# A two-layer decoder trunk on one core: waits moved between ScalarE, VectorE and GpSimd in the mixer

## The chip, the cores and the metric

The kernel runs on one core of a Trainium2 chip. A core has five engines, each with its own in-order queue of instructions: TensorE (PE in the profile; its weight loads are PEld), VectorE (DVE), ScalarE (ACT), GpSimd (POOL) and SyncE (SP, which here only issues loads). They wait for one another by semaphores. Matrix products are written to PSUM banks, and PSUM is emptied by DVE or ACT. The metric is the time on the device of one execution, in microseconds (us); lower is better.

## The reference

A decoder trunk of 2 layers on 256 tokens of width 1024, everything in float32. Each layer is x + half a SwiGLU, then a mixer, then x + half a second SwiGLU:

```python
for l in range(DEPTH):
    x = x + 0.5 * swiglu_ffn(x, ffn1_norm[l], ffn1_w_gu[l], ffn1_w_down[l])      # 1024 -> 2 x 2816 -> 1024
    h = rms_norm(x, mix_norm[l])
    x = x + hybrid_mixer(h, ...)
    x = x + 0.5 * swiglu_ffn(x, ffn2_norm[l], ffn2_w_gu[l], ffn2_w_down[l])
# hybrid_mixer: h @ w_in, cut into columns for three causal attentions
o_a = stick_breaking_attention(...)   # 4 heads
o_b = nsa_attention(...)              # 8 query heads, 2 kv groups: compressed, selected and window branches
o_c = dsa_attention(...)              # 4 query heads, one kv head; relu indexer of 8 heads picks 64 keys a token
merged = g_a * (o_a @ w_br_a) + g_b * (o_b @ w_br_b) + g_c * (o_c @ w_br_c)      # g = sigmoid(h @ w_gate)
return merged @ w_out
```

Queries and keys of NSA and DSA are normalized per head (an RMS norm over 64 columns) and get a rotation on their first 16 columns; the indexer's queries and key get a rotation on 8 of 32 columns, without a norm.

## The kernel before, in words

The activations lie transposed (128 features by 256 tokens a tile). Every weight matrix streams through once in **units** of 128x1024: SP loads a unit into one of four `raw` buffers, ACT rounds it to a high part `wh` (L242), DVE, or for some units GpSimd, subtracts to get a low part `wl` (L244), and PE multiplies with both. PE's work of a unit is written two units after its load is (`LA = 2`): `unit` appends it to `ahead`, `run_unit` takes it from there.

The order of each engine is the order in which the program writes instructions, somewhat rearranged by the scheduler of the framework; PE's own order is pinned by `nosync` links, one matmul after the other. Between units run **threads**: Python generators that `spawn` registers and that `tick` resumes once a unit; `yield n` means to write on after n units. So a `yield` isn't a wait of the chip: it sets how many units' instructions stand between two pieces of a thread.

In the mixer the units are, in this order (`ORDER`): group 0 of w_in (indexer, DSA's value), the compressed keys' two units, group 3 (keys and DSA's queries), a gate pair, group 4 (NSA's queries `q8`), a gate pair, group 1 (stick-breaking's q and k, `p4`), group 2, then the rest of the gates. A group of w_in needs two `acc` banks of PSUM, a gate one; there are three `acc` banks, two `sc` (scores), two `tp` (transposes and small sums) and one `o`.

The threads that matter here: `indexer` (scores by matmuls, relu L742 on ACT into `rl`, weighted sums `isc` on DVE L746 and L748, then eight rounds of MAX and MATCH_REPLACE, L757 and L758, on both token halves); `keys` and `queries` (`norm_rope`: squares on ACT, their sums on DVE, a root by `head_rsqrt` as a logarithm and an exponential on ACT, L501, with a Newton step on DVE; two multiplications on DVE, L676 and L679; then `rope`: three products L648 to L650, of which L649 is on GpSimd, and a sum L652). `keys` then splits each key in two parts (`stack_k`: ACT L699, GpSimd L700), transposes them on PE and copies them out (`kSW` L784 on ACT, `kD` by `evens` on ACT L635 or DVE L637). `queries` does that with L880 (ACT) and L881 (DVE). `group` empties the `acc` banks (L526 on ACT: `p4` of group 1). `dsa` and `nsa_unit` are the attentions over these, written into the gates' units. `first_norm` and `norm_rstd` make the first norm's 1/rms: sums by a matmul, a root on DVE, a broadcast by a second matmul of `dg`.

The list `slow` names the units of a mixer, counted from its first, whose `wl` GpSimd makes.

Of the kernel before, what the change touches and what calls it, by code (L numbers as in the profile page):

```python
# [9 lines left out]
F32 = mybir.dt.float32  # L10
# [4 lines left out]
ALU = mybir.AluOpType  # L15
AX = mybir.AxisListType

P = 128
D = 1024
S = 256  # L20
NT = 2
# [93 lines left out]
M0 = 7  # L115
FY2 = 2
ACC = 3
SC = 2
TP = 2
# [4 lines left out]
def decoder_trunk(ctx: ExitStack, tc: tile.TileContext, x_in, consts, gains, hgain, gu1, dn1, win, wkc, wgate, cw1, cw2,  # L124
# [17 lines left out]
    def nm(s):  # L142
        cnt[0] += 1
        return f"{s}_{cnt[0]}"
# [243 lines left out]
    def rsqrt(src, n, inv):  # L388

        u, y, w = (small.tile([P, 32], F32, tag=t, bufs=2, name=nm(t))[:, 0:n] for t in "uyw")  # L390
        V.tensor_scalar(out=u, in0=src, scalar1=inv, scalar2=EPS, op0=ALU.mult, op1=ALU.add)
        V.tensor_scalar(out=y.bitcast(I32), in0=u.bitcast(I32), scalar1=-0.5, scalar2=float(0x5f3759df), op0=ALU.mult,
                        op1=ALU.add)
        for _ in range(3):
            V.tensor_tensor(out=w, in0=y, in1=y, op=ALU.mult)
            V.scalar_tensor_tensor(out=w, in0=w, scalar=-0.5, in1=u, op0=ALU.mult, op1=ALU.mult)
            V.scalar_tensor_tensor(out=y, in0=w, scalar=1.5, in1=y, op0=ALU.add, op1=ALU.mult)
        return y
# [91 lines left out]
    def mixer(l, nrm, nxt):  # L490
# [47 lines left out]

        gate, iw = st([NT, 24], "gate", 2, "gate"), st([NT, 8], "iw", 2, "iw")
        rq = st([NT], "rq", 2, "rq")  # L540
# [99 lines left out]
        def rope(v, nh, half, cs, sn):  # L640
# [7 lines left out]
            V.tensor_tensor(out=a, in0=v[:, :, :, 0:2 * half], in1=cb, op=ALU.mult)  # L648
            G.tensor_tensor(out=b[:, :, :, 0:half], in0=v[:, :, :, half:2 * half], in1=sb[:, :, :, 0:half], op=ALU.mult)  # L649
            V.tensor_tensor(out=b[:, :, :, half:2 * half], in0=v[:, :, :, 0:half], in1=sb[:, :, :, half:2 * half],  # L650
# [3 lines left out]
        def head_rsqrt(ss, n):  # L654

            u, y, w = (st([32], t, 2, t)[:, 0:n] for t in "uyw")
            V.tensor_scalar(out=u, in0=ss, scalar1=1.0 / HD, scalar2=EPS, op0=ALU.mult, op1=ALU.add)
            act_exp(out=y, in_=u, func=AF.Ln)
            act_exp(out=y, in_=y, scale=-0.5)
# [5 lines left out]
        def norm_rope(v, nh, gs, t0=0):  # L665

            nt = v.shape[1]
            ss = st([32], "hs", 2, "hs")[:, 0:nt * nh]
            for t in range(nt):
                sq = b4("sq")[:, 0:nh * HD].rearrange("p (h d) -> p h d", d=HD)  # L670
                A.activation(out=sq, in_=v[:, t], func=AF.Square)
                V.tensor_reduce(out=ss[:, t * nh:(t + 1) * nh], in_=sq, axis=AX.X, op=ALU.add)
            yield 1
            r = head_rsqrt(ss, nt * nh).rearrange("p (a b) -> p a b", b=nh)
            yield 1
# [127 lines left out]
        def compress():  # L803
# [49 lines left out]
            A.activation(out=junk, in_=kc, func=AF.Square, accum_out=css)  # L853
            yield 1
            rc = head_rsqrt(css, 1)
            V.scalar_tensor_tensor(out=kc, in0=kc, scalar=rc, in1=hg[:, 5 * HD:6 * HD], op0=ALU.mult, op1=ALU.mult)
# [17 lines left out]
        def queries():  # L874
            yield from need(4)
            parts = [norm_rope(q8[t][:, :, HD:P].unsqueeze(1), 8, ((0, 8, 3),), t) for t in range(NT)]
            for _ in zip(*parts):
                yield 1
            for t in range(NT):
                A.activation(out=q8[t][:, :, 0:HD].bitcast(F32R), in_=q8[t][:, :, HD:P], func=AF.Copy)  # L880
                V.tensor_tensor(out=q8[t][:, :, HD:P], in0=q8[t][:, :, HD:P], in1=q8[t][:, :, 0:HD], op=ALU.subtract)  # L881
            yield 4
            for t in range(NT):
# [54 lines left out]
        def dsa():  # L938
            yield from need("mdsa", "qD")
            for t in range(NT):  # L940
# [11 lines left out]
                yield 1  # L952
                o = psum("tp", TP)
                for b in range(t + 1):
# [142 lines left out]
        gates = iter(range(12))  # L1097
        slow.extend(int(u in (10, 14, 18, 27)) for u in range(62))
        for g in ORDER:
# [75 lines left out]
    def first_norm():  # L1175
        for m in range(KD):
# [3 lines left out]
            if m == 6:  # L1180
                nc.sync.dma_start(out=cst, in_=consts)
        yield 2
        yield from norm_rstd(nrm, FY2)
# [83 lines left out]
```

## Time and profile before

| | us |
|---|---|
| median of three runs | 1226.95 (1223.9 to 1229.97) |
| the profiled execution: its time | 1228.48 |
| its span, first to last instruction | 1226.7 |
| PE busy in the span | 1206.3 |
| DVE, ACT, POOL busy | 886.6, 697.6, 163.4 |
| loads: 209 MB read, mean | 171 GB/s |

A row of the order of time reads: start, duration, engine, line, operation, result <- operands, shape, count of merged instructions, and in brackets how long the engine was idle before it and what ended that. Matmuls overlap, so the next row of PE starts some 0.25 us before the end that is shown for the one before. A row of stretches gives, for each engine, busy time and in brackets the count, and then PE's granted clock (1.00 is full).

### The profile page before, as it was taken

How to read it: one execution, taken by the hardware profiler on the slowest of the kernel's cores; microseconds unless marked ns; L12 is line 12 of the kernel's file. 1: busy time of each engine (PE TensorE's matmuls, PEld its weight loads, DVE VectorE, ACT ScalarE, POOL GpSimd, SP SyncE). 2: the span in 40 equal slices, each digit the busy share in tenths (PEclk: the TensorE clock that was granted, in tenths of full speed). 3: DMA queues.
4: the chain of work that ended last, by engine and by line, in shares of the span. 5: the costliest groups of instructions: out<-in, count | busy, mean ns of one | idle time of the engine just before them, and what ended most of it. 6: DMA issues, size and time to landing. Idle time of an engine off the chain costs nothing.

```text
span 1226.7 us, 20872 instructions
## 1 busy us (share of the span) xinstructions
PE 1206.3 (98%) x7878; PEld 1075.5 (88%) x7878; DVE 886.6 (72%) x1563; ACT 697.6 (57%) x1261; POOL 163.4 (13%) x195
## 2 busy tenths in 40 slices
PE   8999999989999999999999999999999999999998
PEld 7888888878989988888888888897798899888887
DVE  7766677896766877766777766778877578776664
ACT  6655555555666565555556555545556745655542
POOL 2111011330000111110111110122300001111100
PEclk9999999999999999999999999999999999999999
DMA  7555566644334565556656655665433346555563
GB/s 265 178 188 184 179 188 193 213 145 131 106 102 141 177 193 191 191 185 182 189 182 196 191 186 184 191 197 192 139 127 112 104 148 195 181 192 190 186 198 104
DMA packets 60885, 212.09 MB, mean 173 GB/s; under 512 B 6992, under 2 KB 8048, under 8 KB 60784
## 3 DMA queue, kind: packets, MB, share of 16 engines
q1 hardware_dynamic: 60192, 209.65, 53.7%
q0 software_dynamic: 448, 1.08, 0.4%
q8 instruction: 62, 1.02, 0.3%
q14 instruction: 39, 0.32, 0.1%
q10 hardware_dynamic: 144, 0.02, 0.0%
HBM read 209.15 MB, written 1.05 MB: 171 GB/s over the span
## 4 chain that ended last, share of the span: by engine, by line
PE 89%; DVE 6%; DMA 2%; ACT 1%; POOL 1%; issue 1%; SPq 0%; ACTq 0%; DVEq 0%; POOLq 0%
PE acc L196 67%; PE sc L196 17%; PE tp L689 2%; DVE wl L244 2%; PE o L196 1%; DMA raw<-in_win 1%; DVE isc L758 1%; PE tp L196 1%; DVE m L757 1%; ACT wh L242 1%; DVE isc L748 1%; DMA gn<-in_gains 0%; POOL rb L649 0%; DVE p L679 0%; DVE isc L746 0%
## 5 line engine op out<-in xcount | busy, mean ns | idle before, releaser
L242 ACT ACTIVATE wh<-raw 128x1024 fp32r<-128x1024 f32 (+4 forms) x402 | 412.1, 1027 | 412.4 <-PE acc L196 285.6
L244 DVE TENSOR_TENSOR wl<-raw,wh 128x1024 fp32r<-128x1024 f32 (+3 forms) x394 | 468.3, 1191 | 221.5 <-ACT wh L242 220.4
L196 PE MATMUL acc<-aT,wh 128*128 128x512 f32 (+1 forms) x1696 | 414.1, 342 | 1.1 <-ACT wh L242 1.1
L196 PEld LDWEIGHTS acc<-aT,wh 128*128 128x128 f32 x1696 | 264.9, 189 | 41.0 <-ACT wh L242 1.5
L196 PE MATMUL acc<-aT,wl 128*128 128x256 f32 x1280 | 297.1, 280 | 0.7 <-DVE wl L244 0.7
L196 PE MATMUL acc<-hT,wh 128*128 128x512 f32 (+1 forms) x792 | 239.1, 369 | 0.0
L196 PEld LDWEIGHTS acc<-aT,wl 128*128 128x128 f32 x1280 | 215.9, 189 | 3.0 <-DVE wl L244 2.0
L196 PE MATMUL sc<-aT,wh 128*128 128x512 f32 x544 | 190.8, 395 | 0.0
L196 PE MATMUL acc<-hT,wl 128*128 128x256 f32 x704 | 186.6, 283 | 0.0
L196 PEld LDWEIGHTS acc<-hT,wh 128*128 128x128 f32 x792 | 137.4, 188 | 26.9
L196 PE MATMUL sc<-aT,wl 128*128 128x256 f32 x544 | 150.6, 278 | 0.0
L196 PEld LDWEIGHTS acc<-hT,wl 128*128 128x128 f32 x704 | 127.1, 188 | 0.0
L442 POOL TENSOR_TENSOR v<-v,R 128x256 f32<-128x256 f32 x88 | 68.2, 779 | 414.3 <-DVE v L358 359.9
L196 PEld LDWEIGHTS sc<-aT,wh 128*128 128x128 f32 x544 | 101.8, 188 | 23.6
L196 PEld LDWEIGHTS sc<-aT,wl 128*128 128x128 f32 x544 | 102.3, 188 | 0.4
L386 POOL TENSOR_TENSOR ssum<-ssum,sq 128x256 f32<-128x256 f32 x42 | 38.3, 912 | 449.1 <-ACT sq L385 448.9
L196 PE MATMUL acc<-wh,aT 128*128 128x512 f32 (+1 forms) x320 | 83.9, 404 | 4.6 <-ACT p L526 4.6
L196 PEld LDWEIGHTS acc<-wh,aT 128*128 128x128 f32 x320 | 59.3, 194 | 15.9 <-ACT p L526 5.5
L357 ACT ACTIVATE half<-acc 128x256 f32<-128x256 f32 x136 | 49.4, 365 | 2.6 <-PE acc L196 1.8
L444 DVE TENSOR_TENSOR v<-v,v 128x256 f32<-128x256 f32 x88 | 38.4, 440 | 12.1 <-ACT v L443 4.3
L376 DVE SCALAR_TENSOR_TENSOR aT<-x,gn,aT 128x256 fp32r<-128x256 f32 x48 | 40.5, 853 | 6.9 <-ACT aT L375 6.9
L501 ACT ACTIVATE E<-sc,mx 128x128 f32<-128x128 f32 (+1 forms) x80 | 32.6, 418 | 21.8 <-DVE mx L905 21.7
(241 smaller groups left out, 1262.8 us busy)
## 6 DMA issues: line engine op xcount, KB each, us to landing
raw<-in_gu SPq DMA_DIRECT2D x175, 512.0 KB, 3.7
raw<-in_dn SPq DMA_DIRECT2D x64, 512.0 KB, 3.5
raw<-in_wgate SPq DMA_DIRECT2D x48, 512.0 KB, 3.4
raw<-in_win SPq DMA_DIRECT2D x32, 512.0 KB, 3.5
raw<-in_dn SPq DMA_DIRECT2D x32, 384.0 KB, 3.0
raw<-in_wbr SPq DMA_DIRECT2D x16, 512.0 KB, 3.4
raw<-in_wout SPq DMA_DIRECT2D x16, 512.0 KB, 3.5
raw<-in_cw SPq DMA_DIRECT2D x8, 512.0 KB, 4.5
```

The lines of the kernel that those rows point to most:

```text
L196: return pe(T.matmul(o, lhsT=lhsT, rhs=rhs, start=start, stop=stop, skip_group_check=True))
L242: A.activation(out=wh[:, w], in_=raw[:, w], func=AF.Copy)
L244: e.tensor_tensor(out=wl[:, w], in0=raw[:, w], in1=wh[:, w].bitcast(F32), op=ALU.subtract)
L357: A.activation(out=t, in_=b[:, S:2 * S], func=AF.Copy)
L376: V.scalar_tensor_tensor(out=dst[:, m, 1], in0=xs[m], scalar=g[:, m:m + 1], in1=dst[:, m, 0].bitcast(F32), op0=ALU.mult, op1=ALU.subtract)
L386: G.tensor_tensor(out=ssum, in0=ssum, in1=sq, op=ALU.add)
L442: G.tensor_tensor(out=g, in0=g, in1=N["R"], op=ALU.mult)
L444: V.tensor_tensor(out=u, in0=u, in1=g, op=ALU.mult)
L501: e = A.activation(func=func, **kw)
L689: pe(T.transpose(tp[:, b * P:(b + 1) * P], src, ident))
L748: V.scalar_tensor_tensor(out=isc[t], in0=rl[:, j], scalar=w, in1=isc[t], op0=ALU.mult, op1=ALU.add)
L757: V.max(out=m8, in_=isc[t])
```

## The change

Six edits.

1. `head_rsqrt` becomes a generator with a `yield 1` behind the scaled sum u (L657): the logarithm and the exponential on ACT are written one unit later than u. In `norm_rope` and `compress` the `yield 1` that stood ahead of u goes. The buffers of u, y and w become 3, 4 and 2 of 18 columns (2 of 32 before).
2. `queries`: two units (`yield 2`) more stand ahead of the copies and subtractions (L880, L881), two less behind them.
3. `rope`: the first of the two sine products (L649) goes from GpSimd to DVE.
4. `dsa`: the sums over the values go to an `acc` bank instead of a `tp` bank.
5. `slow`: of four units of a mixer (10, 14, 18, 27) only 27 keeps its `wl` on GpSimd.
6. The first norm: one unit less ahead of its sum's matmul (`yield 1`), one more between that and the broadcast (`FY2 = 3`).

```diff
-FY2 = 2
+FY2 = 3
...
-        u, y, w = (small.tile([P, 32], F32, tag=t, bufs=2, name=nm(t))[:, 0:n] for t in "uyw")
+        u, y, w = (small.tile([P, 18], F32, tag=t, bufs={'u': 3, 'y': 4, 'w': 2}[t], name=nm(t))[:, 0:n] for t in "uyw")
...
-        gate, iw = st([NT, 24], "gate", 2, "gate"), st([NT, 8], "iw", 2, "iw")
+        gate, iw = st([NT, 24], "gate", 1, "gate"), st([NT, 8], "iw", 1, "iw")
...
-            G.tensor_tensor(out=b[:, :, :, 0:half], in0=v[:, :, :, half:2 * half], in1=sb[:, :, :, 0:half], op=ALU.mult)
+            V.tensor_tensor(out=b[:, :, :, 0:half], in0=v[:, :, :, half:2 * half], in1=sb[:, :, :, 0:half], op=ALU.mult)
...
         def head_rsqrt(ss, n):
 
-            u, y, w = (st([32], t, 2, t)[:, 0:n] for t in "uyw")
+            u, y, w = (st([18], t, {'u': 3, 'y': 4, 'w': 2}[t], t)[:, 0:n] for t in "uyw")
             V.tensor_scalar(out=u, in0=ss, scalar1=1.0 / HD, scalar2=EPS, op0=ALU.mult, op1=ALU.add)
+            yield 1
             act_exp(out=y, in_=u, func=AF.Ln)
...
                 V.tensor_reduce(out=ss[:, t * nh:(t + 1) * nh], in_=sq, axis=AX.X, op=ALU.add)
-            yield 1
-            r = head_rsqrt(ss, nt * nh).rearrange("p (a b) -> p a b", b=nh)
+            r = (yield from head_rsqrt(ss, nt * nh)).rearrange("p (a b) -> p a b", b=nh)
...
-            yield 1
-            rc = head_rsqrt(css, 1)
+            rc = yield from head_rsqrt(css, 1)
...
             for _ in zip(*parts):
                 yield 1
+            yield 2
             for t in range(NT):
                 A.activation(out=q8[t][:, :, 0:HD].bitcast(F32R), in_=q8[t][:, :, HD:P], func=AF.Copy)
                 V.tensor_tensor(out=q8[t][:, :, HD:P], in0=q8[t][:, :, HD:P], in1=q8[t][:, :, 0:HD], op=ALU.subtract)
-            yield 4
+            yield 2
...
-                o = psum("tp", TP)
+                o = psum("acc", ACC)
...
-        slow.extend(int(u in (10, 14, 18, 27)) for u in range(62))
+        slow.extend(int(u == 27) for u in range(62))
...
-        yield 2
+        yield 1
         yield from norm_rstd(nrm, FY2)
```

How the instructions move on the engines, at three places of the first mixer (the second is alike). ACT's queue at the indexer's second token half (`rl` is the relu of a bank of scores, `kk` the high part of the split keys, `hs` an exponential of the compressed keys):

```order
-L699 ACTIVATE kk_2712<-p_401_2152 128x4x128
 L742 ACTIVATE rl_2675<-sc_2672 128x512
 L742 ACTIVATE rl_2682<-sc_2679 128x512
 L501 ACTIVATE hs_519_2688<-o_2448 128x60
+L699 ACTIVATE kk_2712<-p_401_2152 128x4x128
 L699 ACTIVATE kc_524_2715<-p_401_2152 128x128
```

The split of the keys moved behind two relus and the exponential.

ACT's queue from the roots of the compressed keys and the queries (`y`) to the emptying of group 1 (`p`), before:

```order
L242 ACTIVATE wh_2926<-raw_2924 128x1024
L501 ACTIVATE y_2804<-u_2803 128x1
L501 ACTIVATE y_2804<-y_2804 128x1
L242 ACTIVATE wh_2970<-raw_2968 128x1024
L501 ACTIVATE y_2861<-u_2860 128x8
L784 ACTIVATE kSW_2164<-tp_2944 128x4x128
L501 ACTIVATE y_2861<-y_2861 128x8
L784 ACTIVATE kSW_2164<-tp_2950 128x4x128
L242 ACTIVATE wh_3005<-raw_3003 128x1024
```

and with the change:

```order
L242 ACTIVATE wh_2926<-raw_2924 128x1024
L501 ACTIVATE y_2758<-u_2757 128x1
L501 ACTIVATE y_2804<-u_2803 128x8
L501 ACTIVATE y_2812<-u_2811 128x8
L501 ACTIVATE y_2758<-y_2758 128x1
L501 ACTIVATE y_2804<-y_2804 128x8
L501 ACTIVATE y_2812<-y_2812 128x8
L242 ACTIVATE wh_2970<-raw_2968 128x1024
L784 ACTIVATE kSW_2164<-tp_2944 128x4x128
L784 ACTIVATE kSW_2164<-tp_2950 128x4x128
L242 ACTIVATE wh_3001<-raw_2999 128x1024
```

The six roots stand together ahead of one wh, and the two copies of keys behind it. Further on, the query copies (L880) stand a place earlier against the wh's: the second one, which stood right ahead of the four p's (L526), has now one wh between itself and them.

DVE's queue from the first to the second sum of the queries' rotation (L652 of `q_402` and `q_403`, the two token halves), before:

```order
L637 CAST kD_2165<-tp_2986 128x2x128
L660 TENSOR_TENSOR w_2871<-y_2870 128x8
L648 TENSOR_TENSOR ra_2956<-q_402_2153,cst 128x128
L661 SCALAR_TENSOR_TENSOR w_2871<-w_2871,u_2869 128x8
L650 TENSOR_TENSOR rb_2957<-q_402_2153,cst 128x8x8
L662 SCALAR_TENSOR_TENSOR y_2870<-w_2871,y_2870 128x8
L244 TENSOR_TENSOR wl_3006<-raw_3003,wh_3005 128x1024
L676 TENSOR_TENSOR q_403_2154<-q_403_2154,y_2870 128x8x64
L652 TENSOR_TENSOR q_402_2153<-ra_2956,rb_2957 128x8x16
L679 TENSOR_TENSOR q_403_2154<-q_403_2154,hg_2139 128x8x64
L244 TENSOR_TENSOR wl_3034<-raw_3031,wh_3033 128x1024
L648 TENSOR_TENSOR ra_2962<-q_403_2154,cst 128x128
```

and with the change:

```order
L650 TENSOR_TENSOR rb_2957<-q_402_2153,cst 128x8x8
L244 TENSOR_TENSOR wl_2971<-raw_2968,wh_2970 128x1024
L652 TENSOR_TENSOR q_402_2153<-ra_2956,rb_2957 128x8x16
L637 CAST kD_2165<-tp_2986 128x2x128
L648 TENSOR_TENSOR ra_2962<-q_403_2154,cst 128x128
L649 TENSOR_TENSOR rb_2963<-q_403_2154,cst 128x8x8
L650 TENSOR_TENSOR rb_2963<-q_403_2154,cst 128x8x8
L244 TENSOR_TENSOR wl_3002<-raw_2999,wh_3001 128x1024
L652 TENSOR_TENSOR q_403_2154<-ra_2962,rb_2963 128x8x16
L244 TENSOR_TENSOR wl_3030<-raw_3027,wh_3029 128x1024
L881 TENSOR_TENSOR q_402_2153<-q_402_2153 128x8x64
L881 TENSOR_TENSOR q_403_2154<-q_403_2154 128x8x64
```

With the change kD, an emptying of a transpose bank, stands behind a wl and the sum of the first half; L649 is in the queue; the Newton steps (L660 to L662, with the change L661 to L663), which stood between the pieces of the rotation, come earlier; one wl instead of two stands between the two sums, and both subtractions (L881) stand behind the second sum, the first one no longer ahead of it. Three pairs of the top-k's rounds (`m_608` and `m_609` the first of them), which stood further up in this queue, follow behind L881.

More of the change, by code (lines that the diff above doesn't have):

```diff
@@ L667, in norm_rope @@
             nt = v.shape[1]
-            ss = st([32], "hs", 2, "hs")[:, 0:nt * nh]
+            ss = st([18], "hs", 2, "hs")[:, 0:nt * nh]
             for t in range(nt):
```

## The prediction

> **What bounds the kernel now.** I read the busy line first, then the stretches, then TensorE's (PE's) order of time at the waits, then the queue that each wait leads to.
>
> ```profile
> PE 1206.3 (98%) x7878; PEld 1075.5 (88%) x7878; DVE 886.6 (72%) x1563; ACT 697.6 (57%) x1261; POOL 163.4 (13%) x195
> ```
>
> PE sets the end, so only PE's lost time can be won. The stretches (columns: start:end, length, then busy us and count of PE, weight loads, DVE, ACT, POOL; then granted clock, DMA share, GB/s) say where it is lost:
>
> ```profile
> 20.00:135.00 115.00, 114.03 (x649) 98.83 (x648) 83.25 (x144) 69.03 (x126) 15.65 (x21) 1.00 0.59 189
> 232.70:275.50 42.80, 38.50 (x232) 31.83 (x232) 42.17 (x113) 24.14 (x48) 15.64 (x12) 1.00 0.51 166
> 300.00:383.00 83.00, 82.25 (x718) 75.99 (x719) 54.14 (x114) 56.31 (x131) 0.00 (x0) 1.00 0.37 117
> 838.30:881.10 42.80, 39.23 (x226) 32.27 (x224) 42.21 (x112) 24.46 (x48) 15.70 (x12) 0.96 0.52 168
> ```
>
> In the FFN and in the attention PE has no gap worth a term (bar one of about 1 us in each). In 43 us of each mixer it idles, and there DVE is the full engine: 42.2 of 42.8 us. PE's order of time there, first mixer, then second:
>
> ```profile
> 240.13 2.07 PE L196 MATMUL acc<-wh,aT 128*128 128x512 f32 x8
> 244.54 0.51 PE L196 MATMUL sc<-ikS,iqS 128*128 128x256 f32 x2 [1.44 <-ACT rl L742]
> 248.73 2.10 PE L196 MATMUL acc<-wh,aT 128*128 128x512 f32 x8
> 251.59 1.03 PE L689 MATMUL tp<-cst,kk 128*128 128x128 f32 x8
> 252.38 2.16 PE L196 MATMUL acc<-aT,wh 128*128 128x256 f32 x16
> 255.33 0.38 PE L689 MATMUL tp<-cst,kc 128*128 128x128 f32 x2
> 265.91 0.44 PE L689 MATMUL tp<-cst,kc 128*128 128x128 f32 x2 [0.93 <-ACT kSW L784]
> 276.93 1.94 PE L196 MATMUL acc<-wh,aT 128*128 128x512 f32 x6 [2.31 <-ACT p L526]
> 283.69 1.04 PE L689 MATMUL tp<-cst,q 128*128 128x128 f32 x8
> ...
> 845.31 2.09 PE L196 MATMUL acc<-wh,aT 128*128 128x512 f32 x8
> 850.19 0.51 PE L196 MATMUL sc<-ikS,iqS 128*128 128x256 f32 x2 [1.88 <-ACT rl L742]
> 882.56 2.93 PE L196 MATMUL acc<-wh,aT 128*128 128x512 f32 x6 [2.31 <-ACT p L526]
> 889.14 1.03 PE L689 MATMUL tp<-cst,q 128*128 128x128 f32 x8
> ```
>
> An undisturbed unit of 512 columns (12 matmuls) takes 248.73 to 251.59, 2.86 us; eight transposes 0.79; a gate unit 252.38 to 255.33, 2.95. From 240.13 to 283.69 stand nine such units, two gate units, two eights of transposes and seven small groups (some 2.3 us together, by 0.3 to 0.4 each): 25.7 + 5.9 + 1.6 + 2.3 = 35.5. PE took 43.56: **8.1 us lost**. The same work in mixer two took 43.83: **8.3 lost**. Idle time alone is less, since a waiting row costs some 0.25 beyond what is shown idle, and since part is lost at a lower clock:
>
> ```profile
> 240.57:243.98 3.41, 2.53 (x12) 1.76 (x10) 3.31 (x6) 0.61 (x2) 1.27 (x2) 1.00 0.57 193
> 274.70:278.12 3.42, 1.19 (x5) 1.02 (x6) 3.21 (x8) 2.57 (x6) 0.46 (x1) 1.00 0.50 158
> 278.12:281.53 3.41, 3.41 (x10) 2.65 (x9) 0.89 (x2) 1.06 (x1) 0.00 (x0) 0.50 0.49 156
> 848.14:851.56 3.42, 1.54 (x8) 1.21 (x8) 3.27 (x6) 2.54 (x6) 1.83 (x2) 1.00 0.44 144
> 851.56:854.97 3.41, 3.41 (x11) 2.67 (x10) 3.41 (x9) 1.98 (x3) 0.32 (x1) 0.50 0.35 135
> 878.86:882.28 3.42, 1.15 (x7) 0.69 (x6) 3.21 (x9) 2.41 (x6) 1.93 (x1) 1.00 0.73 253
> 882.28:885.69 3.41, 3.13 (x7) 2.49 (x8) 1.50 (x3) 1.61 (x5) 0.00 (x0) 0.50 0.50 160
> ```
>
> Three times 3.41 us at half clock follow 3.41 us in which PE was busy 1.2 to 1.5; after 2.53 busy none follows. They hold 10, 11 and 7 matmuls where 14.3 fit at 2.86 for twelve: at 0.238 each 1.0, 0.8 and 1.7 us. So the 16.4 hold about 3.5 that comes from the clock.
>
> **The change part by part.** Each wait is a queue standing behind ACT:
>
> ```profile
> 243.37 0.63 ACT L699 ACTIVATE kk<-p 128x512 fp32r<-128x512 f32 x1 [3.05 <-DVE p L652]
> 265.16 0.21 ACT L501 ACTIVATE y<-u 128x8 f32<-128x8 f32 x1 [3.44 <-DVE c2s L856]
> 275.52 0.63 ACT L880 ACTIVATE q<-q 128x512 fp32r<-128x512 f32 x1 [1.01 <-DVE q L652]
> 276.06 0.46 ACT L526 ACTIVATE p<-acc,rq 128x256 f32<-128x256 f32 x1
> ```
>
> *Wait at 244.54.* The indexer's relu (L742), which frees the score bank, stood behind the key split L699, which waits for the rotation's last sum (L652). In the new order two relus and the exponential stand ahead of L699: the relu needs only matmuls that end before 240.13, PE comes at 243.1, the wait is gone. Queued behind L699 is now the wh of a gate unit, due on PE some 6 us later.
>
> *Wait at 265.91.* ACT stood at a root (L501) until DVE came to its sum (u, L657); behind it stood the kSW copy that frees a transpose bank. Now all three u's stand on DVE ahead of their roots, right behind a unit's wl, and ACT comes to the six roots with the kSW copies behind them: gone, if DVE is on time.
>
> *Wait at 276.93.* PE needs the bank that p (L526) empties; p stood behind the second half's query copy (L880), that one behind L652 on DVE, whose end is 275.5. This chain stays, so DVE's sum decides. Rows for it:
>
> ```profile
> 222.13 0.29 DVE L746 TENSOR_SCALAR isc<-rl,iw 128x128 f32<-128x128 f32 x1 [2.17 <-ACT rl L742]
> 223.16 2.42 POOL L244 TENSOR_TENSOR wl<-raw,wh 128x1024 fp32r<-128x1024 f32 x1
> 231.66 1.06 ACT L242 ACTIVATE wh<-raw 128x1024 fp32r<-128x1024 f32 x1 [1.69 <-DMA raw<-in_win]
> 239.14 2.35 DVE L746 TENSOR_SCALAR isc<-rl,iw 128x256 f32<-128x256 f32 x1
> 242.48 0.29 DVE L650 TENSOR_TENSOR rb<-p,cst 128x144 f32<-128x144 f32 x1
> 253.85 0.61 DVE L757 MAX8 m<-isc 128x8 f32<-128x128 f32 x2
> 255.02 0.61 DVE L757 MAX8 m<-isc 128x8 f32<-128x128 f32 x2
> ...
> 846.79 0.34 DVE L746 TENSOR_SCALAR isc<-rl,iw 128x256 f32<-128x256 f32 x1
> L244 DVE TENSOR_TENSOR wl<-raw,wh 128x1024 fp32r<-128x1024 f32 x10 | 12.4, 1240 | 1.7 <-ACT wh L242 1.7
> ```
>
> Between the wl at 232.7 and that L652 the new order differs so. Added: wl of units 14 and 18 from GpSimd, while the wl of a later unit moves behind: one net, 1.2. Three first halves of rotations (L649) by L650's row, 0.29 and twice half of it: 0.5. Gone: L746 took 2.35 beside GpSimd's unit and 0.34 in the other mixer, where L679 met it instead: 2.0. Of the top-k, two rounds of both halves and most of a third move behind L652; a round is 253.85 to 255.02, 1.17, so 3.1; they are needed only by the DSA scores, behind all of this. The first half's subtraction (L881) moves behind: 0.9 with its wait; the wait for GpSimd's rotation, 0.2. And the start: DVE stands idle 2.17 before 222.13, so unit 10's wl is done there by about 222.6 instead of 225.6 on GpSimd; its raw buffer, and SP's queue behind it, get free 3 us sooner, and the wh of 231.66, which waited 1.69 for that load, can start up to 1.7 sooner (bounds 0 and 1.7; I take 1.6, since three us of head start exceed the wait). Sum: 275.5 - 1.6 + 1.2 + 0.5 - 2.0 - 3.1 - 0.9 - 0.2 = 269.4. Then ACT's copy, one wh and two p's, 2.0: PE goes on at 271.4. By its own work PE, with the earlier waits gone, is there at about 270.2. So 1.2 of the 8.1 stay: the gain is 6.9. Mixer two starts its DVE chain about 0.3 later against PE: 8.3 - 1.5 = 6.8. With 1.2 late the gate windows stay over 2 us busy: no half clock.
>
> GpSimd keeps at most 15.6 less two units of 2.4, 10.8 us, in this stretch (and loses its rotations). How much of it DVE will wait out isn't shown; it lies between none, with which PE waits for nothing, and all. Of what it meets now only the 2.0 at L746 goes; what is left, 1.5 at most by the other long rows there, stays in my sum, since the same key splits stay on GpSimd.
>
> **The small edits**, each bounded by its own wait:
>
> ```profile
> 29.86 0.70 PE L196 MATMUL tp<-dg,cst 128*128 128x256 f32 x2 [0.97 <-DVE dg L409]
> 362.14 0.66 PE L689 MATMUL tp<-cst,E 128*128 128x128 f32 x4 [0.75 <-ACT PT L929]
> ```
>
> The first norm's sums come a unit (2.8 us) earlier, their broadcast stays: 1.0 won; GpSimd's chain of squares ends before that unit begins, so nothing new is late. DSA's sums leave the transposes' two banks: 0.75 and 0.15 of tail in each mixer, 1.8; the product bank taken is asked for again two gate units later, 5.9 us, and is emptied by four short copies. Buffers of u, y, w, gate, iw: nothing; three roots of y and two of u are live at once in the new order and find three and four. Sum: 6.9 + 6.8 + 1.0 + 1.8 = 16.5, at most 19.2. From the profiled execution's 1228.48: 1212.0. The median of the three runs stands 1.5 below it, so 1210.5 to 1212: **1211**.
>
> **The rivals.** *DVE takes PE's waits (0.18).* For: it is full, and two-input operations beside GpSimd ran long (L746, L679). Against: most of them didn't. Half of GpSimd's 10.8 met instead of 1.5 delays PE by 3.9 in each mixer: 16.5 - 7.8 gives 1219. By the Trainium skill, "SBUF — State Buffer", section "Who interferes with whom", a VectorE instruction with two SBUF inputs shares GpSimd's read port, an exclusive lock: that speaks for this rival.
>
> *The half clock stays (0.10).* Then its 3.5 us aren't the waits' doing: 16.5 - 3.5 gives 1214. For: it would need another cause, such as power; against: all three follow an idle stretch. The Trainium skill, "TensorE: Matmul & The Clock Gate", section "HAM oscillation — how this bites in real kernels", asks for "no PE-idle gaps >~3.4µs": by that rule these gaps, 2.3 us at most, wouldn't close the gate. The trace differs: it closed after 1.9 to 2.3 idle in 3.41.
>
> *Slower (0.05).* One mechanism: DVE's chain to L652 ends later than 275.5 instead of 269.4. It takes over 6.1 more on DVE. All of GpSimd's 10.8 met adds 9.3, to 278.7: PE then waits 3.2 longer than now in each mixer, and only the small edits are won: 1228.5 + 6.4 - 2.8 = 1232. It decides from 275.5 on, that is when DVE waits out some two thirds of GpSimd's time.
>
> *The waits only move (0.04).* The loads bound the stretch, and PE stands for raw tiles instead: near 1226. Against: DMA share 0.51 there, and only the wh's of 231 to 237 waited for loads.
>
> **How the numbers follow.** Forecast 0.63, the rest as above. Its own range is 1207.5 (all 19.2 won, less 1.5) to 1215 (no earlier load, 1.6 twice). Taking in the half clock and DVE's case with 2 us behind it, and 1 us of spread below: 1206.5 to 1221. A measurement of this kernel tells 0.5% (6.1 us), so faster means under 1220.8: 0.63 + 0.10 + 0.12 of the 0.18 make 0.85; same 0.10; slower 0.05.
>
> **What would show it.** Right: the waits on rl, kSW and dg gone from PE's rows, the one on p at most 1.5; three clock stretches of 0.50 gone; L746 near 0.34; DVE still full from 232 to 270 and the top-k's last rounds behind it; the second DSA wait gone. Wrong: PE waiting for kD (L637), which now stands behind a unit and half the rotations on DVE and holds a transpose bank: due at 267.5 by the sum, asked at 266.4, inside the 1.2 above. If that wait exceeds 3 us, or the hrep sums come after 246, my order of DVE was too short.

## The result and the profile after

The changed kernel takes 1207.2 us (median of four runs, 1206.65 to 1211.23) against 1228.1 (1223.9 to 1229.97): the ratio is 0.9842, with a 95% interval of 0.9807 to 0.9876. It is faster, by about 19 us after the ratio (20.9 between the medians); 1211 was forecast, in a range of 1206.5 to 1221. Its profiled execution is the slowest of its four, 1211.23 with a span of 1209.5, against 1228.48 and 1226.7 before. So the two traces differ by 17.2 us, and that is what can be followed in them.

The busy line of the changed kernel:

```profile
PE 1197.8 (99%) x7878; PEld 1070.7 (89%) x7878; DVE 884.2 (73%) x1577; ACT 697.9 (58%) x1261; POOL 145.8 (12%) x181
```

PE is now idle for 11.7 us of the span instead of 20.4. The stretches that answer to those of before, each mixer's full part from the unit ahead of it (columns as before: length, busy us of PE, weight loads, DVE, ACT, POOL, then granted clock, DMA share, GB/s):

```profile
20.00:135.00 115.00, 114.55 (x652) 99.31 (x651) 82.49 (x144) 69.42 (x127) 18.36 (x22) 1.00 0.59 190
229.90:270.60 40.70, 38.53 (x255) 33.05 (x254) 38.69 (x102) 25.04 (x49) 7.79 (x7) 1.00 0.53 175
827.30:866.30 39.00, 37.55 (x253) 32.47 (x252) 37.74 (x102) 24.38 (x48) 7.78 (x7) 1.00 0.55 176
300.00:383.00 83.00, 83.00 (x724) 77.12 (x724) 55.27 (x108) 55.01 (x122) 0.00 (x0) 1.00 0.36 114
```

GpSimd's time there is halved (7.8 instead of 15.6 us), the clock is 1.00 in both, and the attention has no idle PE any more. DVE is nearly as full as before, 95 and 97% of the stretch. PE's order of time in the changed kernel's mixers, the rows that answer to those of the waits before:

```profile
239.00 2.11 PE L196 MATMUL acc<-wh,aT 128*128 128x512 f32 x8
241.87 0.40 PE L196 MATMUL sc<-ikS,iqS 128*128 128x256 f32 x2
245.68 0.63 PE L196 MATMUL o<-w,hrep 128*128 128x64 f32 x4 [0.70 <-ACT wh L242]
267.24 0.41 PE L689 MATMUL tp<-cst,kc 128*128 128x128 f32 x2 [1.47 <-DVE kD L637]
270.59 2.48 PE L196 MATMUL acc<-wh,aT 128*128 128x512 f32 x8
276.54 1.03 PE L689 MATMUL tp<-cst,q 128*128 128x128 f32 x8
...
864.60 0.41 PE L689 MATMUL tp<-cst,kc 128*128 128x128 f32 x2 [1.46 <-DVE kD L637]
```

The waits on rl (241.87), on kSW and on p (270.59: some 0.4 longer than an undisturbed eight, no more) are gone. A new one stands in each mixer, 1.47 and 1.46 on DVE's copy of kD, and the first mixer has one of 0.70 ahead of the sums with hrep. The stretch that took 43.56 us, from the unit at 240.13 to the transposes at 283.69, now goes from 239.00 to 276.54: 37.54. Setting the starts of the same matmuls of both traces beside each other, the 17.2 us divide so: start 0.6, first mixer 5.9, second mixer 7.4, attention 1.6 in both layers together, and 1.7 in the rest, where no queue and no wait of the change lies.

What DVE did, changed kernel:

```profile
238.24 0.35 DVE L746 TENSOR_SCALAR isc<-rl,iw 128x256 f32<-128x256 f32 x1 [1.14 <-ACT rl L742]
266.48 0.28 DVE L652 TENSOR_TENSOR q<-ra,rb 128x128 f32<-128x128 f32 x1
266.68 0.41 DVE L637 CAST kD<-tp 128x256 fp32r<-128x256 f32 x1
268.62 0.28 DVE L652 TENSOR_TENSOR q<-ra,rb 128x128 f32<-128x128 f32 x1
```

The second L652, which the prediction's sum put at 269.4, ends at 268.90. PE's whole program runs 1.1 earlier by then, so in the time of the trace before it is 270.0.

### The profile page after: what moved, and what is told of

Same layout as the page of the kernel before. It is cut to its first block, busy times and chain, and to the rows that moved or that the text cites. A ratio compares the mean times of both kernels' runs of the same rounds, so it can differ in the third digit from the quotient of the medians.

```text
span 1209.5 us, 20859 instructions
## 1 busy us (share of the span) xinstructions
PE 1197.8 (99%) x7878; PEld 1070.7 (89%) x7878; DVE 884.2 (73%) x1577; ACT 697.9 (58%) x1261; POOL 145.8 (12%) x181
## 5 line engine op out<-in xcount | busy, mean ns | idle before, releaser
L244 DVE TENSOR_TENSOR wl<-raw,wh 128x1024 fp32r<-128x1024 f32 (+4 forms) x400 | 473.9, 1187 | 211.5 <-ACT wh L242 210.6
L196 PE MATMUL acc<-hT,wh 128*128 128x512 f32 (+1 forms) x792 | 236.2, 367 | 0.0
L196 PE MATMUL acc<-wh,aT 128*128 128x512 f32 (+1 forms) x320 | 81.1, 394 | 0.2
L358 DVE TENSOR_TENSOR v<-acc,half 128x256 f32<-128x256 f32 x108 | 44.7, 417 | 1.5 <-ACT half L357 1.5
```

Source lines behind the costliest of these rows:

```text
L196: return pe(T.matmul(o, lhsT=lhsT, rhs=rhs, start=start, stop=stop, skip_group_check=True))
L244: e.tensor_tensor(out=wl[:, w], in0=raw[:, w], in1=wh[:, w].bitcast(F32), op=ALU.subtract)
L358: V.tensor_tensor(out=o, in0=b[:, 0:S], in1=t, op=ALU.add)
```

## The experiments

Twelve kernels were run. Each was run beside the kernel before, whose median was 1225.4 to 1226.5 in these runs and 1228.1 beside the changed kernel; so the ratios are the safer comparison. Two of the twelve, `p_late` and `shifted_32`, were executed once and have no ratio; they stand further down.

| kernel | median us | ratio, 95% interval | PE's waits in the two mixers |
|---|---|---|---|
| changed | 1207.2 | 0.9842 (0.9807 to 0.9876) | kD 1.47, 1.46 |
| undo_units | 1217.1 | 0.9929 (0.9912 to 0.9945) | rl 1.91, 0.23 and 1.37; kD 2.49, 2.51 |
| undo_buffers | 1207.8 | 0.9858 (0.9843 to 0.9872) | p 0.26 in the second |
| undo_query_yields | 1208.2 | 0.9862 (0.9847 to 0.9876) | kD 0.32, 1.46 |
| undo_rope | 1208.0 | 0.9862 (0.9847 to 0.9877) | kD 1.66, 1.66 |
| undo_small | 1211.5 | 0.9880 (0.9865 to 0.9895) | kD 0.80, 0.63 |
| only_units | 1218.7 | 0.9943 (0.9923 to 0.9963) | p 2.31, 2.30; qD 0.26, 0.24; kc 0.21 |
| only_buffers | 1222.2 | 0.9964 (0.9951 to 0.9977) | rl 0.96, 0.67 and 1.37; kD 2.94, 2.95 |
| aligned | 1211.1 | 0.9876 (0.9857 to 0.9894) | kD 0.35, 1.46 |
| kd_on_act | 1208.6 | 0.9849 (0.9833 to 0.9866) | p 0.76, 1.53; qD 0.17 |
| undo_buffers_same_place | 1206.1 | 0.9834 (0.9820 to 0.9849) | p 0.29, 0.31 |

Waits on hrep's unit, 0.4 to 0.7 where they occur, and three of 0.19 to 0.35 on DVE at the start of the second mixer (`undo_units`, `only_buffers`) are left out of the table.

### One edit undone

`undo_buffers` (edit 1):

```diff
-            u, y, w = (st([18], t, {'u': 3, 'y': 4, 'w': 2}[t], t)[:, 0:n] for t in "uyw")
+            u, y, w = (st([18], t, 2, t)[:, 0:n] for t in "uyw")
...
-            yield 1
             act_exp(out=y, in_=u, func=AF.Ln)
...
+            yield 1
             r = (yield from head_rsqrt(ss, nt * nh)).rearrange("p (a b) -> p a b", b=nh)
```

> The changed kernel with edit 1 undone: u, y and w have two buffers each again, and the yield stands ahead of u again. (With the yield alone put back and the buffers kept, every engine's order is the one of the changed kernel, so the buffers are what edit 1 does to the order.) Theory (each wait is a queue, and the roots' place decides two of them): the third u is written on DVE behind the first root's Newton step, the roots are spread over four wh on ACT, the kSW copies stand behind them, and DVE has one more wl ahead of the second L652. PE waits about 0.9 for kSW again in each mixer, the second L652 ends near 271 to 272 instead of 268.9, p's bank makes PE wait 1.5 to 2.5. Time 1211 to 1214 against 1207 for the changed kernel. Rival (GpSimd's units alone did it): 1207 to 1208, no wait on kSW.

No change that can be told: 1207.8. PE waits neither for kSW nor for kD, and 0.26 for p in the second mixer. ACT's and DVE's rows in `undo_buffers` show why (the line of L880 is 882 there):

```profile
258.60 0.21 ACT L501 ACTIVATE y<-u 128x8 f32<-128x8 f32 x1 [1.79 <-DVE c2s L857]
258.71 0.58 ACT L785 ACTIVATE kSW<-tp 128x512 fp32r<-128x512 f32 x1
262.56 0.41 DVE L637 CAST kD<-tp 128x256 fp32r<-128x256 f32 x1
266.78 0.46 ACT L526 ACTIVATE p<-acc,rq 128x256 f32<-128x256 f32 x1
267.75 0.28 DVE L652 TENSOR_TENSOR q<-ra,rb 128x128 f32<-128x128 f32 x1
268.68 0.66 ACT L882 ACTIVATE q<-q 128x512 fp32r<-128x512 f32 x1
```

The root stands ahead of kSW again and waits 1.79 (3.44 before), but it is done at 258.8, and PE isn't kept. And p comes at 266.78, ahead of the second L652: with the query copies two units later, the second L880 (L882 here) stands behind the four p's, so p doesn't wait for the second rotation. What I had put down to the roots' place, kSW's wait, is gone without it, and the theory that it decides p falls.

`undo_units` (edit 5):

```diff
-        slow.extend(int(u == 27) for u in range(62))
+        slow.extend(int(u in (10, 14, 18, 27)) for u in range(62))
```

> The changed kernel with edit 5 undone: wl of units 10, 14 and 18 on GpSimd again. Theory: in the new order L699 (kk) stands ahead of two relus on ACT again, so PE waits 1.4 to 1.9 for rl in each mixer, with one half clock stretch behind it in the second; L746 or a neighbour on DVE takes about 2.3 again beside the GpSimd unit; the wh near 231 waits for its load again. Against it DVE has 2.4 us less of wl. Time 1210 to 1213. Rival (these units cost nothing where GpSimd has room, DVE's shorter queue pays): 1205 to 1207.

9.9 us come back by the medians, more than either theory said. PE's waits and the work beside them in `undo_units`:

```profile
241.99 0.51 PE L196 MATMUL sc<-ikS,iqS 128*128 128x256 f32 x2 [1.91 <-ACT rl L742]
268.27 0.41 PE L689 MATMUL tp<-cst,kc 128*128 128x128 f32 x2 [2.49 <-DVE kD L637]
...
235.80 3.03 DVE L679 TENSOR_TENSOR p<-p,hg 128x128 f32<-128x128 f32 x3
235.62 2.39 POOL L244 TENSOR_TENSOR wl<-raw,wh 128x1024 fp32r<-128x1024 f32 x1 [13.09 <-ACT wh L242]
...
840.23 2.22 DVE L746 TENSOR_SCALAR isc<-rl,iw 128x256 f32<-128x256 f32 x1 [0.17 <-ACT rl L742]
```

The parts of the mechanism are back: the wh of 228.34 waits 1.41 for its load, kk (L699) stands ahead of the relus in ACT's queue, DVE's operations beside a GpSimd unit are stretched (three L679 take 3.03, in the changed kernel 0.95; L746 2.22 against 0.35), and DVE's later chain makes kD late by a microsecond more. The Trainium skill, "SBUF — State Buffer", section "Who interferes with whom", has VectorE's second read port shared with GpSimd under an exclusive lock; these rows agree: beside a GpSimd unit of 2.39 us the operations of DVE are stretched by some 2 us. (L679 has two tensors as inputs. L746 has one and a column of factors; the rows don't show which port it holds.) Both mixers have a half clock stretch again. It follows right behind the waits for kD, 2.49 and 2.51, and not a wait on rl, as expected; neither theory had a term for these waits and their half clock.

`undo_query_yields` (edit 2; the lines on yields) and `undo_rope` (edit 3; the last):

```diff
-            yield 2
             for t in range(NT):
                 A.activation(out=q8[t][:, :, 0:HD].bitcast(F32R), in_=q8[t][:, :, HD:P], func=AF.Copy)
...
-            yield 2
+            yield 4
...
-            V.tensor_tensor(out=b[:, :, :, 0:half], in0=v[:, :, :, half:2 * half], in1=sb[:, :, :, 0:half], op=ALU.mult)
+            G.tensor_tensor(out=b[:, :, :, 0:half], in0=v[:, :, :, half:2 * half], in1=sb[:, :, :, 0:half], op=ALU.mult)
```

> The changed kernel with edit 2 undone (no yield ahead of the query copies, yield 4 behind them). In the order the second L880 stands ahead of a copy of qD, and the first L881 ahead of the second L652, in place of nothing else. Theory (DVE's chain up to the second L652 sets p): L652 0.6 later by L881, p 0.3 to 0.6 later, PE waits about 1 for it: 1208 to 1209. Rival (the later copies are what takes p out of the way): p waits 2 or more again, a half clock behind it, 1211 to 1214.

> The changed kernel with edit 3 undone: L649 on GpSimd again (172 to 145 us less on DVE isn't the matter; three short products per mixer go). In the order the first L652 and kD come ahead of a wl each. Theory: DVE has 0.7 less ahead of the second L652, GpSimd's rotation makes it wait 0.2 to 0.5, kD comes 1.2 earlier: PE's 1.47 wait for kD shrinks to under 0.5: 1205 to 1207, so this edit gains nothing. Rival (GpSimd's short product takes DVE's shared time, as L746 and L679 showed): 1209 or more, waits on L652.

Neither can be told from the changed kernel. `undo_query_yields` has the time that its theory gave, 1208.2, but by luck: the wait of about 1 on p that was to make it isn't there. The rotation's engine is worth nothing that can be told; kD's wait stayed (1.66), though I expected it below 0.5.

`undo_small` (edits 4 and 6):

```diff
-FY2 = 3
+FY2 = 2
...
-                o = psum("acc", ACC)
+                o = psum("tp", TP)
...
-        yield 1
+        yield 2
         yield from norm_rstd(nrm, FY2)
```

> The changed kernel with edits 4 and 6 undone (DSA's sums in a transpose bank, the first norm's sum and broadcast where they were). Both theories: the waits on dg (0.97) and on the transposes behind PT (0.75 and 0.15 of tail, twice) are back, 2.8 us, 1209 to 1211 against 1207. Rival: the DSA wait was made by what stood around it before, and doesn't come back: 1208.

The two waits are back with the sizes of before (0.96 on dg, 0.75 behind PT in each layer). By the starts of the matmuls it is 0.6 + 1.0 + 1.0 = 2.6 us; the medians differ by 4.3, with intervals of 1.8 us to either side here and 4.2 for the changed kernel.

### One edit alone

Both are the kernel before with these lines, the first pair in `only_units`, the second in `only_buffers` (with the same in the first norm, and gate, iw and hs in the sizes of the changed kernel, so that they fit):

```diff
-        slow.extend(int(u in (10, 14, 18, 27)) for u in range(62))
+        slow.extend(int(u == 27) for u in range(62))
...
-            u, y, w = (st([32], t, 2, t)[:, 0:n] for t in "uyw")
+            u, y, w = (st([18], t, {'u': 3, 'y': 4, 'w': 2}[t], t)[:, 0:n] for t in "uyw")
```

> The kernel before with edit 5 alone: wl of units 10, 14 and 18 on DVE instead of GpSimd. After the first runs (undoing this edit cost 10 us, undoing the buffers, the queries' yields or the rotation's engine cost less than 1) the theory is: GpSimd's units alone were what made DVE late, and the other edits of the mixer are worth nothing together. Then this kernel has all of the gain but the small edits (start 1.0, DSA 0.9 twice): 1209 to 1211 against 1207. Rival, my prediction's sum (the roots' place, the queries' copies and the units each carry a part): 1215 to 1219, with waits of 0.9 on kSW and 1 or more on p left.

> The kernel before with edit 1 alone, as buffers (three of u, four of y; the yield changes no engine's order): the roots stand together, GpSimd keeps its units. Theory (units alone): waits on rl, and kD or p, stay; 1222 to 1226 against 1225 to 1228 for before. Rival, my prediction's sum: kSW's wait and most of p's are gone, 1217 to 1221.

By the medians they are 7.7 and 4.2 us below before, of about 19. `only_units` took 1218.7: in the rival's range, not in the theory's, though without the wait on kSW that the rival expected. `only_buffers` took 1222.2, the lower end of the theory's range, with waits on rl and kD as the theory had it, but without those on kSW and p, as the rival had it. `only_units`, the place of p's wait:

```profile
271.01 0.29 DVE L652 TENSOR_TENSOR q<-ra,rb 128x128 f32<-128x128 f32 x1 [0.21 <-POOL rb L649]
271.33 0.63 ACT L880 ACTIVATE q<-q 128x512 fp32r<-128x512 f32 x1 [1.00 <-DVE q L652]
271.87 0.46 ACT L526 ACTIVATE p<-acc,rq 128x256 f32<-128x256 f32 x1
272.75 2.77 PE L196 MATMUL acc<-wh,aT 128*128 128x512 f32 x6 [2.31 <-ACT p L526]
```

The units alone (edit 5) take away the waits on rl and on kSW, and L652 ends 4.2 us sooner than before (271.3 for 275.5). But PE comes 4 us sooner too, and waits for p the same 2.31 us, with the same half clock behind it. To be rid of that wait one of two things is needed: L880 out of p's way (edit 2, as in `undo_buffers`) or the second rotation in time (edit 1, as in `undo_query_yields`). Either is enough, so undoing one costs nothing, and with neither the wait stays. In `only_buffers` p's wait and kSW's are gone while GpSimd keeps its units; in their place PE waits 2.94 for kD, since the buffers let both halves' roots go ahead and kD falls behind a wl and half a rotation on DVE:

```profile
270.09 0.66 PE L689 MATMUL tp<-cst,kc 128*128 128x128 f32 x2 [2.94 <-DVE kD L637]
...
874.98 0.41 PE L689 MATMUL tp<-cst,kc 128*128 128x128 f32 x2 [2.95 <-DVE kD L637]
```

So the new wait on kD comes with edit 1, and with all six edits it is half as long.

### The new wait taken away

`kd_on_act`:

```diff
-                evens(out=kD[:, :, s], in_=heads(tp))
+                A.activation(out=kD[:, :, s], in_=heads(tp), func=AF.Copy)
```

> The changed kernel with both copies of kD on ACT (before, the first of a mixer on ACT, the second on DVE, behind a wl and the rotations). Theory (PE's 1.47 wait in each mixer is kD's place in DVE's queue): ACT stands idle 2.99 ahead of the first query copy there, so kD is done about when PE asks: the wait is gone in both mixers, 2 to 3 us less, 1204 to 1205. Rival (ACT's copy pushes the query copy and p, whose bank PE waits for next): the gain is half of that or none, 1206 to 1208.

The rival was right: kD's wait is gone from both mixers and p's is back, 0.76 and 1.53, no gain. These rows are of `kd_on_act`:

```profile
269.13 1.65 PE L196 MATMUL acc<-wh,aT 128*128 128x512 f32 x6 [0.76 <-ACT p L526]
866.42 1.66 PE L196 MATMUL acc<-wh,aT 128*128 128x512 f32 x6 [1.53 <-ACT p L526]
```

### The half clock

`p_late` was to make PE wait with nothing else changed:

```diff
-                        evac(p4[:, t, 0:256], b[:, 0:256], rq[:, t:t + 1], A)
+                        for _ in range(13 if t == 0 else 1):
+                            evac(p4[:, t, 0:256], b[:, 0:256], rq[:, t:t + 1], A)
```

> The changed kernel with the first emptying of group 1 (L526) written 13 times instead of once, into the same place: PE gets its bank 12 times 0.36, so 4.3 us or more later in each mixer, with nothing else changed. Theory (the clock is halved for 3.41 us after 3.41 us in which PE was busy less than half, as in all runs so far: 1.63 and less halved, 1.75 and more not): one half clock stretch in each mixer at least, and 1 to 2 us of it each beside the wait: 1207 + 8.6 + 2 to 4 = 1218 to 1220. Rival (the half clock goes with something else of the kernel before, such as DVE and GpSimd at work together): no half clock, 1215 to 1216.

It took 1211.34 in its one execution and says nothing on the clock: the repeated copies were spread between the others on ACT, PE waited only 0.85 in each mixer, and no 3.41 us there had PE busy for less than 2.3. So no run made for it tests the rule; it is read from the traces. The clock's records lie on a grid of 3.41 us, and in all fourteen traces together, without the programs' last stretches, 25 stretches of the grid have PE busy for 2.31 us or less. The nine lowest, 0.92 to 1.63, are each followed by one at half clock; the sixteen others, from 1.75 up, by none. The two nearest to the boundary, in `undo_buffers` (at the start, with loads late; 1.62 by the rounded ends of the row) and in `undo_rope`:

```profile
3.89:7.30 3.41, 1.62 (x23) 1.41 (x21) 1.13 (x3) 1.68 (x5) 0.00 (x0) 1.00 0.95 306
7.30:10.71 3.41, 3.41 (x13) 2.89 (x12) 2.92 (x7) 3.41 (x10) 1.57 (x2) 0.50 1.02 407
```

```profile
861.54:864.95 3.41, 1.75 (x11) 1.33 (x10) 3.41 (x7) 2.66 (x6) 1.39 (x2) 1.00 0.47 135
864.95:868.37 3.42, 3.30 (x17) 2.46 (x16) 3.42 (x11) 2.55 (x6) 0.00 (x0) 1.00 0.82 248
```

The length of a wait alone doesn't decide. In `only_buffers` PE waits 2.94 for kD in the first mixer and 2.95 in the second. Of the first, 2.3 us lie in one stretch of the grid, and half clock follows; the second is split, 1.6 and 1.3 us, between two stretches with 1.79 and 2.08 busy, and none follows:

```profile
266.08:269.49 3.41, 1.07 (x7) 0.68 (x5) 3.41 (x7) 1.70 (x3) 2.58 (x3) 1.00 0.00 0
269.49:272.91 3.42, 2.82 (x8) 2.37 (x9) 3.42 (x7) 1.23 (x3) 0.03 (x1) 0.50 0.55 158
870.24:873.65 3.41, 1.79 (x10) 1.25 (x8) 3.41 (x9) 1.29 (x3) 2.14 (x2) 1.00 0.19 78
873.65:877.06 3.41, 2.08 (x10) 1.79 (x11) 3.41 (x8) 1.83 (x4) 0.77 (x2) 1.00 0.53 154
```

### Where the tiles lie

`aligned` and `shifted_32` add unused bytes and move no instruction:

```diff
+    small.tile([P, 8], F32, tag="spad", bufs=1, name="spad")      # both
+    cpool.tile([P, 8], F32, tag="pad", name="pad")                # aligned alone
```

> The changed kernel with 32 unused bytes ahead of the weights' buffers and 32 ahead of the small ones; no engine's order changes. In the traces a matmul of a SwiGLU's down part (moving hT) takes 233 and 120 ns in the kernel before and in undo_buffers, where hT begins 32 bytes behind a multiple of 64, and 230 and 118 ns in the changed kernel and the three other runs, where it begins on one. aT, wh and wl begin 32 behind a multiple of 64 in all of them, with 230 to 236 ns. Theory (the place of an operand modulo 64 sets the pace): with all of them on multiples of 64 the up parts' and the mixer's matmuls get 1 to 2% faster, some 600 us of PE: 1195 to 1202. Rival (what sets the pace is another thing that goes with the buffers, such as which of the two aT tiles is used): within 2 of the changed kernel.

> The changed kernel with 32 unused bytes among the small tiles: hT and all behind it lie 32 bytes further, as they do modulo 64 in the kernel before; aT, wh and wl stay. No engine's order changes. If the place of hT and what is behind it modulo 64 set the pace, every stretch of the SwiGLU parts runs as in the kernel before: 233 and 120 ns in the down parts, 232 and 115 in the up part after the first mixer. If it is the distance in another sense, it is neither.

`undo_buffers_same_place` is `undo_buffers` with one unused tile more:

```diff
+            kept_.append(small.tile([P, 72], F32, tag="pad", bufs=1, name="pad"))
```

> undo_buffers with 288 unused bytes behind the small tiles, so that every tile but u, y and w begins where it does in the changed kernel; no engine's order differs from undo_buffers. Theory (where the tiles lie sets PE's pace, not the order): a matmul of the down parts takes 230 and 118 ns again as in the changed kernel, those of the second layer's first up part 236 and 117 as there; PE's waits in the mixers are those of undo_buffers, none on kD. Sum by the traces: 0.5 to 1.5 below undo_buffers, 1205.5 to 1207. Rival (the order sets the pace): 233 and 120 in the down parts, the time of undo_buffers.

The same stretch of the program in four traces, from one matmul of the second layer's first up part to another (first row of each) and the same in the down part behind it (second row); the first number is the length. Kernel before:

```profile
639.03:717.72 78.69, 78.69 (x455) 68.84 (x454) 56.88 (x89) 46.95 (x86) 11.28 (x14) 1.00 0.61 194
752.30:790.80 38.50, 38.50 (x221) 33.74 (x220) 26.74 (x36) 19.59 (x31) 4.28 (x4) 1.00 0.60 187
```

Changed kernel:

```profile
630.02:710.23 80.21, 80.21 (x456) 69.51 (x454) 56.50 (x89) 46.79 (x86) 11.27 (x14) 1.00 0.60 191
745.11:783.12 38.01, 38.01 (x221) 33.45 (x220) 26.77 (x36) 19.62 (x31) 4.31 (x4) 1.00 0.61 190
```

`undo_buffers_same_place`:

```profile
627.80:708.00 80.20, 80.20 (x455) 69.59 (x454) 56.50 (x89) 46.77 (x86) 11.25 (x14) 1.00 0.60 191
742.88:780.90 38.02, 38.02 (x221) 33.47 (x220) 26.79 (x36) 19.63 (x31) 4.31 (x4) 1.00 0.61 190
```

`shifted_32`:

```profile
629.87:708.57 78.70, 78.70 (x456) 68.77 (x455) 56.92 (x90) 46.97 (x86) 11.21 (x14) 1.00 0.61 194
743.22:781.97 38.75, 38.75 (x222) 33.66 (x221) 26.80 (x36) 19.60 (x31) 4.30 (x4) 1.00 0.60 188
```

PE is busy throughout in all of them at clock 1.00, with the same matmuls, and still takes 78.69 or 80.21 us, and 38.0, 38.5 or 38.75. The order isn't the cause: with the tiles' places of the changed kernel, the order of `undo_buffers` runs at the changed kernel's pace to 0.01 us, while `undo_buffers` itself runs at that of before (78.69 and 38.49). So edit 1 moved the pace of PE by moving every tile behind the small ones: this stretch of the second layer's first up part lost 1.5 us, the down parts won 1.3% each. My rule for it, places modulo 64 bytes, was wrong: `aligned`, in which aT, wh, wl and hT all begin on multiples of 64, runs like `shifted_32` (78.69 and 38.75), gained nothing and took 1211.1 where I expected 1195 to 1202 (the rival's 2 us around the changed kernel was missed too, by the medians); and `shifted_32`, with hT 32 behind a multiple of 64 as before, doesn't run like before in the down part. What the two have in common is the distance from aT to hT (41152 bytes; 41120 in the changed kernel; 41344 and 40832 with the pace of before). Whether that distance is the cause, or that to some other tile, stays open. `shifted_32` took 1211.45 in its one execution.

## Why the prediction was right, and where not

The forecast, its sign and its mechanism held: the waits went, the three half clock stretches with them, and the time came out inside the range, 4 us below the number. That the sum of its terms, 16.5, lies so near to the 17.2 between the two traces is in part luck: its terms together gave 15.5 (5.9 for 6.9 in the first mixer, 7.4 for 6.8 in the second, 2.2 for 2.8 by the small edits), and 1.7 came from where it had no term. By the prediction's own steps:

- **The wait on rl.** Gone, as worked out, by L699's place behind the relus. The runs add which edit does it: GpSimd's units (gone in `only_units`, back in `undo_units`, still there in `only_buffers`).
- **The wait on kSW.** Gone, but the step's reason, "ACT comes to the six roots with the kSW copies behind them", is one of two that are each enough. With it alone the wait goes (`only_buffers`). But in `only_units` and `undo_buffers` the roots stand as before, and PE doesn't wait for kSW either: with DVE in time the copy behind the root is early enough. Nor is the generator's yield what places the roots: with the yield put back where it was and the buffers kept, every engine's order is that of the changed kernel, so the order comes from the third u and the third and fourth y. I had costed these buffers at nothing.
- **The wait on p.** The chain L652, L880, p was read rightly, and L652's end was forecast to 0.6 us. What the sum didn't see is that edit 2 takes p off the second rotation even without the buffers (`undo_buffers`), and that the two cures overlap. Hence the 10 us of undoing the units, and nothing for undoing either of the others.
- **The term for the earlier load, 1.6.** It held for the wh that it was worked out for, and what it won was lost again two units later. Rows of the changed kernel:

```profile
223.72 0.33 SPq L148 DMA_DIRECT2D raw<-in_win  x1
...
228.59 1.06 ACT L242 ACTIVATE wh<-raw 128x1024 fp32r<-128x1024 f32 x1
232.71 1.06 ACT L242 ACTIVATE wh<-raw 128x1024 fp32r<-128x1024 f32 x1 [2.24 <-DMA raw<-in_win]
236.66 1.06 ACT L242 ACTIVATE wh<-raw 128x1024 fp32r<-128x1024 f32 x1 [2.41 <-DMA raw<-in_win]
```

SP issued the load some 1.0 us earlier against PE than before (226.03, with 1.3 us between the programs here), and it landed 2.0 us earlier. The wh that had waited 1.69 for it (231.66 before) starts at 228.59 without a wait, 1.8 us sooner against PE. In `undo_units` and `only_buffers`, where GpSimd keeps its units, the first mixer's wh waits for this load again, 1.41 and 1.23. But the wh's of the two units behind it still stood 2.24 and 2.41 for their loads, and L746 1.14 for the relu behind the second of them, so L746 starts 0.2 later against PE than before. That second load took 5.4 us from issue to landing; in `aligned` and `shifted_32`, with the same order, it took 3.8 and 3.3, and the wh waited 1.04 and 0.51.

That the sum for L652 still came within 0.6 is in part luck. From L746 to the end of the second L652 DVE took 30.7 us instead of 36.4: 5.7 less, where the sum's terms without the load give 4.5. L746 (2.35 to 0.35) and the top-k (3.2 less; its last rounds now stand behind L881) held. The 1.2 beyond the terms are 0.3 at the added wl and some 0.9 in rows that had no term, such as L648 (0.75 to 0.45), L838 (0.45 to 0.18) and the seven L748 (0.3 together). They made up for most of what the late load took.

- **kD.** The prediction named it as what could go wrong, with 1.2 us of it inside the sum; it was 1.47. The same order had 0.35 and 0.48 there in the first mixer of `aligned` and `shifted_32`, where the load above came in time. `kd_on_act` shows that this wait isn't the last: behind it stands p.
- **The half clock.** Gone in the changed kernel, and back in both mixers of `undo_units` and `only_units` and in the first of `only_buffers`, each time behind a wait of 2.3 to 2.9. Not every wait brings it back: the shorter ones of the table don't, nor does the 2.95 that is split between two stretches. The rival that it stays is refuted.
- **The small edits.** 2.8 forecast, 2.2 by the traces (0.6 and 1.6) and 2.6 by undoing them: the start's new order leaves a wait of 0.45 on a wl at 38.4.
- **What had no term.** 1.7 us of the 17.2 come from PE's pace in the parts that the change doesn't touch, by the places of the tiles.

The rival with GpSimd wasn't what happened, but its mechanism belongs to the case. Edit 5 took away three things at once: the rows stretched beside GpSimd's units, L699's place ahead of the relus, and the late load ahead of a wh. No run takes these three apart, so how much of the 8 to 10 us each of them carries stays open.

And the 4 us between forecast and median: the profiled execution, beside which the sum was set, is 4.2 above the median of the other three. In its first mixer it spent 2.0 us more than `aligned` and `shifted_32`, which have the same order; the rows above show the load that landed late, and L746 and kD late behind it. Its first up part took 1.8 us longer than the same part in `undo_buffers` and `undo_units`, though no longer than in the eleven other traces. That these two make the 4 us isn't shown, as the other executions have no trace.

No version beats the changed kernel by more than can be told. `undo_buffers_same_place` is the lowest, 1206.1, with an interval that overlaps. It does show that edit 1's third and fourth buffers can go: its mixers have no wait above 0.31.

## What to carry to other kernels

Undo each part as well as trying each alone: here two parts were worth 4 and 8 us alone, one 10 and the other nothing when undone, because each of two edits could cure the same wait. A queue's wait that disappears is replaced by the next one in time (rl, then p or kD), so price an edit by where the engine is asked next, not by the wait that it removes. When buffers' numbers or sizes change, compare PE's length over stretches without a wait: the places of the tiles can move it by 1 to 2%, either way.

## What the runs showed of the hardware

The granted clock falls to 0.50 for one 3.41 us stretch when PE was busy for less than about half of the stretch before (halved at 1.63 and below, not at 1.75 and above, 25 cases in 14 traces; no run was made that tests it between these). The Trainium skill, "TensorE: Matmul & The Clock Gate", section "HAM oscillation — how this bites in real kernels", gives gaps longer than some 3.4 us as what to avoid; here gaps of 2.3 us and less were enough, as what counted was the sum within a stretch of the grid. By the same count a gap of 2.95 us, split between two stretches, left the clock at 1.00 (`only_buffers`).

PE's pace at full clock, without waits and with the same matmuls, differed by up to 1.9% in a stretch (78.69 and 80.21 us) with the places of tiles in SBUF. It repeats to 0.02 us in all kernels with the same places, in every stretch without a wait behind the first up part. In that first part it also differs between kernels of the same places (`undo_units` went 1.9% faster there than the changed kernel), which no run explains.
